# DeltaNet's triangular inverse: update products that serve two chunks, and a block transposition on VectorE

## The chip, the cores and the metric

The kernel runs on one core of one Trainium2 chip. The metric is the device time of one execution in microseconds; of the kernel before, three executions were timed, 1096.20, 1097.21 and 1097.26, median 1097.21. A further execution was profiled.

## The reference, cut to what matters

One layer of a decoder trunk: RMSNorm, one projection `z = h @ W_in`, four token mixers side by side (HGRN2, mLSTM, windowed attention, gated DeltaNet), a gated merge, an output projection and a squared-ReLU MLP. 512 tokens, model width 1024, all in float32. The change touches the DeltaNet mixer (4 heads, key and value width 128):

```
lower = where(strict, beta * (k k^T) * decay, 0) + I          # unit lower triangular, per chunk and head
sol   = triangular_solve(lower, [v*beta, k*beta*exp(gam)])    # u, w
v_new = u - w @ S;  o = q_dec @ S + attn @ v_new;  S = g_last*S + k_dec^T @ v_new    # chunk after chunk
```

The kernel uses chunks of 128 tokens (4 of them) and forms the inverse of `lower` instead of solving.

## The kernel before, in words

**Streams and tasks.** Every projection is a chain of matmuls whose weights come from memory in pieces (`raw`), are split into two reduced-precision parts `whi` (ScalarE) and `wlo` (VectorE) by `split` (L477), and go through TensorE as three 128x512 products per weight block (`mm3`). These are the streams (`pf`, `pt`, `pbr`, `yo`, `dn` in the profile). Between them lie the mixers' tasks: `dn_pre`, four `dn_head`, four `dn_fin`, four `hg_head` and so on.

**Who sets the order.** No operation is issued where it is written. The wrapper in `wrap` (the call at L223; the matmuls at L434 and transposes at L475) records each operation with an estimated cost; `lay_out` (L231) then plans all engines with these costs, at most `WINDOW = 5` tasks at a time, stream matmuls ranked behind the tasks' matmuls, and tiles taken from a fixed number of slots (`z2`: 37, `pm` in PSUM: 5, `w8`: 4). `emit` issues the operations in the planned order. On the chip each engine runs its list in that order and waits on semaphores.

**The inverse.** `dn_pre` (L930) makes `W` (the negated strict lower part, transposed) for all heads, inverts the 32x32 diagonal blocks by a serial recurrence on VectorE, and puts the result into `U0`, one tile of 16 (head, chunk) blocks of 128x128, named `dnU` in the profile. In `dn_head` (L1018) `U` is the head's part of it: the transposed inverse so far, block diagonal at first, and `Tm` its transpose by 32x32 blocks (`V.transpose`, L1025). Two doublings, n = 32 and n = 64 (L1043), fill in the off-diagonal blocks. Each does, for all four chunks:

- `yp`: four 128x128 float32 products `W^T Tm`; `Yt` is `yp` times a mask (L1045), a VectorE instruction over 128x512;
- `up`: four products `Yt^T U` (L1048); `Un = up + U`, a VectorE instruction over 128x512 into a new tile;
- for n = 32 alone, `tp`: four products `U^T Yt` (L1052) and `Tn = tp + Tm`, so that the transpose follows.

`bank4` (L792) runs the four products of one group into one PSUM bank. A float32 product of 128x128 stands as two MATMUL records in the profile. Behind the doublings comes the scan over the four chunks (`dnt`, `dno`, `dnX`, `dnV`, `dnS`), which uses `U` as an operand. `hg_head` (L1161) fills its 32 and 64 wide blocks with products that serve two chunks, and moves the wanted blocks by VectorE copies over 32 or 64 partitions (`A5`, L1212).

**The end.** `mlp_units` (L1675): the last accumulation group of the down projection is evacuated by two `scalar_tensor_tensor` of 256 columns (L1707), and each half is stored by a DMA that SyncE issues (L1712).

Of the kernel before, what the change touches and what calls it, by code (L numbers as in the profile page):

```python
# [20 lines left out]
P = 128  # L21
# [68 lines left out]
class _Flow:  # L90
# [85 lines left out]
    def wrap(self, key, eng):  # L176
        flow = self

        class W:
            def __getattr__(self, name):  # L180
                fn = getattr(eng, name)

                def call(*a, **k):
                    ops = dict(k)
                    if "out" not in ops:
                        ops["out"], a = a[0], a[1:]
                        call_a = (ops["out"],) + a
                    else:
                        call_a = a
                    out = ops.pop("out")  # L190
                    outs = [out] + ([ops.pop("accum_out")] if "accum_out" in ops else [])
                    ins = [v for v in list(a) + list(ops.values()) if isinstance(v, bass.AP)]
                    n = 1
                    for d in out.shape[1:]:
                        n *= d
                    big = [v for v in ins if v.space == PSUM]
                    table, dma = None, 0
                    if name == "dma_start":
                        dma = n * out.shape[0] * 4
                        c = 1000 if key == "g" else 500 if key == "y" else 60  # L200
                    elif key == "v":
                        if name == "tensor_tensor_scan":
                            c = 65 + 2.09 * n
                        elif name == "reciprocal":
                            c = 65 + 6.26 * n
                        elif name in ("tensor_copy", "tensor_scalar", "memset") and not big:
                            c = 65 + 0.52 * n
                        elif name in ("reduce_sum", "reduce_max"):
                            m = 1
                            for d in ins[0].shape[1:]:  # L210
                                m *= d
                            c = 65 + 1.04 * m
                        else:
                            c = 65 + 1.04 * n
                        if name in ("tensor_scalar", "scalar_tensor_tensor") and len(ins) > (1 if name == "tensor_scalar" else 2):
                            c += 65
                    elif key == "s":
                        f = a[1] if name == "activation" and len(a) > 1 else k.get("func")
                        table = {AF.Exp: "e", AF.Ln: "e", AF.Sigmoid: "s", AF.Silu: "u"}.get(f)
                        c = (52 if big else 92) + 0.833 * n + 95 * ("accum_out" in k) + 93 * sum(isinstance(k.get(x), bass.AP) for x in ("scale", "bias"))  # L220
                    else:
                        c = 110 + n * (0.8 if name == "memset" else 2.15 if len(ins) > 1 else 1.0)
                    flow.record(key, c, lambda: fn(*call_a, **k), outs, ins, table, dma,  # L223
                                two="accum_out" in k)

                return call

        return W()
# [176 lines left out]
def tile_hybrid_parallel_gated_mixers(  # L405
# [62 lines left out]
    def ch(ap, c):  # L468
        return ap[:, c * P:(c + 1) * P]
# [322 lines left out]
    def bank4(name, fn):  # L792
        o = ps(name)
        for c in range(NCH):
            fn(c, ch(o, c))
        return o
# [221 lines left out]
    def dn_head(h):  # L1018
        yield ["dnpre", f"dnv{h}"]
        q, k, v = dn["q"][h], dn["k"][h], dn["v"][h]  # L1020
        col, gl = dn["col"], dn["gl"]
        W = dn["W"][:, 4 * h:4 * h + 4, :]
        U = dn["U0"][:, 4 * h:4 * h + 4, :].rearrange("p c t -> p (c t)")
        Tm = z2("Tm")
        V.transpose(Tm, U)  # L1025
        yield
        ra = row_tile("ra", dn["ra"], h)
        qk = bank4("qk", lambda c, o: mm(o, ch(k, c), ch(q, c)))
        da, qd = z2("da"), z2("qd")
        for c in range(NCH):  # L1030
            stt(ch(da, c), ch(ra, c), col[:, c, h:h + 1], con("minc"), ALU.add, ALU.add)
        act(qd, ra, AF.Exp)
        act(da, da, AF.Exp)
        tt(qd, qd, q, ALU.mult)
        tt(da, qk, da, ALU.mult)
        yield
        kt = transpose4("kt", k)
        kd, bv = z2("kd"), z2("bv")
        tt(c3(kd), c3(kt), col[:, :, 96 + h:97 + h].to_broadcast([P, NCH, P]), ALU.mult)
        vt = transpose4("vt", v)  # L1040
        tt(c3(bv), c3(vt), col[:, :, 64 + h:65 + h].to_broadcast([P, NCH, P]), ALU.mult)
        yield
        for n in (32, 64):  # L1043
            yp = bank4("yp", lambda c, o: mm(o, W[:, c, :], ch(Tm, c)))
            Yt = z2("Yt")  # L1045
            tt(c3(Yt), c3(yp), con4(f"y{n}"), ALU.mult)
            yield
            up = bank4("up", lambda c, o: mm(o, ch(Yt, c), ch(U, c)))  # L1048
            Un = z2("U")
            tt(Un, up, U, ALU.add)  # L1050
            if n < 64:
                tp = bank4("tp", lambda c, o: mm(o, ch(U, c), ch(Yt, c)))  # L1052
                Tn = z2("Tm")
                tt(Tn, tp, Tm, ALU.add)
                Tm = Tn
            U = Un
            yield
        o, tb = ps("dno"), ps("dnt")
        St = None
        for c in range(NCH):  # L1060
            if c == 0:
                X = ch(bv, 0)
            else:
                kS = ch(tb, 0)
                mm(kS, ch(k, c), St)
                X = sq128("dnX")
                stt(X, kS, col[:, c, 32 + h:33 + h], ch(bv, c), ALU.mult, ALU.add)
                yield
            vp = ch(tb, 1)
            mm(vp, ch(U, c), X)  # L1070
            vn = sq128("dnV")
            S.copy(vn, vp)
            yield
            if c < NCH - 1:
                dS = ch(tb, 2)
                mm(dS, ch(kd, c), vn)
                Sn = sq128("dnS")
                if c == 0:
                    V.tensor_copy(Sn, dS)
                else:  # L1080
                    stt(Sn, St, gl[:, h, c:c + 1], dS, ALU.mult, ALU.add)
            if c:
                mm(ch(o, c), St, ch(qd, c), start=True, stop=False)
            mm(ch(o, c), vn, ch(da, c), start=c == 0, stop=True)
            if c < NCH - 1:
                St = Sn
                yield
        dn["on"][h] = yield from head_norm(o)
# [586 lines left out]
    def mlp_units():  # L1675

        for hf in range(NH):
# [11 lines left out]
            for j in range(2):  # L1689
                obox = {}  # L1690
                for kg in range(FH // 4):
                    r0 = (hf * FH + kg * 4) * P
                    subs = []
                    for k2 in range(2):
                        box = {}

                        def view(raw, k2=k2):
                            return raw[:, 2 * k2:2 * k2 + 2, :]

                        def step(k, c, kg=kg, k2=k2, box=box, obox=obox, hf=hf, j=j, ah=ah, al=al):  # L1700
                            kk = kg * 4 + k2 * 2 + k
                            if kk == 0 and c == 0:
                                obox["o"] = [ps("dn") for _ in range(4)]
                            o = obox["o"][c]
                            mm3(o, ch(ah[kk], c), ch(al[kk], c), box["hi"][:, k, :], box["lo"][:, k, :],
                                kk == 0, kk == FH - 1)
                            n = 2 if kk == FH - 1 and hf == NH - 1 and j == 1 and c == 3 else 1  # L1707
                            for a in range(n if kk == FH - 1 else 0):
                                cs = slice(a * T // n, (a + 1) * T // n)
                                stt(acc[c][j][:, cs], o[:, cs], tail["rs2"][:, c:c + 1], acc[c][j][:, cs], ALU.mult, ALU.add)  # L1710
                                if hf == NH - 1:
                                    Y.dma_start(out[c * P:(c + 1) * P, j * T + cs.start:j * T + cs.stop], acc[c][j][:, cs])  # L1712

                        order = [(k, c) for k in range(2) for c in range(4)]
                        if kg == FH // 4 - 1 and k2 == 1:
                            order = [(k, c) for c in range(4) for k in range(2)]
                        subs.append((pieces_k(box, view, 2, T), [lambda k=k, c=c, step=step: step(k, c) for k, c in order],
                                     None))
# [92 lines left out]
```

## Time and profile before

| what | value |
|---|---|
| median of 3 executions | 1097.21 us (1096.20 to 1097.26) |
| profiled execution | 1096.43 us, span from first to last instruction 1094.6 us |
| TensorE busy | 1081.7 us, 99% |
| VectorE, ScalarE, GpSimd busy | 678.4, 535.6, 30.2 us |
| chain that ended last | TensorE 79%, VectorE 12%, ScalarE 5% |

PE is TensorE's matmuls, PEld its weight loads, DVE VectorE, ACT ScalarE, POOL GpSimd, SP SyncE; a q behind the name is an engine's sequencer. Busy time counts a record from its start to its modelled end; matmuls overlap one another, so the distance of their starts, and not the duration of one, says how fast they follow. Back-to-back VectorE instructions overlap too: two of 0.69 us stand as one piece of about 1.28 us.

### The profile page before, as it was taken

The page shows a single profiled execution, that of the slowest core. Times are in us where ns is not written, and L with a number is a line of the kernel's source. Part 1 is how long each engine was busy: PE and PEld are TensorE (multiplying, and loading weights), DVE is VectorE, ACT ScalarE, POOL GpSimd, SP SyncE. Part 2 cuts the span into 40 slices and gives each one's busy share as a digit, 9 for nine tenths or more (in the row PEclk, how much of TensorE's full clock was granted, in tenths as well). Part 3 has the DMA queues.
Part 4 walks back from the last instruction along what each step waited for, and adds up shares of the span by engine and source line. Part 5 has one row for each costly group of instructions (what it writes and reads, how often), then busy time and mean ns, then how long its engine had stood idle before and what let it go on. Part 6 is the DMA issues. An engine that isn't in the chain of part 4 may idle for free.

```text
span 1094.6 us, 14138 instructions
## 1 busy us (share of the span) xinstructions
PE 1081.7 (99%) x5339; PEld 905.9 (83%) x5339; DVE 678.4 (62%) x1417; ACT 535.6 (49%) x970; POOL 30.2 (3%) x69
## 2 busy tenths in 40 slices
PE   8999999999999999999999999999999999999998
PEld 8889888898888888778887888888888888888886
DVE  5765999758999999976387334545443324444232
ACT  5764478226774778776267233345442222443220
POOL 4000000000000001000000010000000000000000
PEclk8999999999999999999999999999999999999999
DMA  6342554515422355222322252323232323232331
GB/s 235 89 107 97 157 182 153 185 49 167 142 87 87 108 170 174 78 78 78 116 78 77 83 186 91 102 77 116 77 116 77 116 77 116 78 115 80 113 116 39
DMA packets 95580, 122.19 MB, mean 112 GB/s; under 512 B 11104, under 2 KB 65844, under 8 KB 95256
## 3 DMA queue, kind: packets, MB, share of 16 engines
q1 hardware_dynamic: 90216, 115.03, 32.3%
q0 software_dynamic: 1984, 5.61, 1.6%
q10 hardware_dynamic: 3312, 0.66, 0.3%
q8 instruction: 42, 0.69, 0.3%
q14 instruction: 26, 0.21, 0.1%
HBM read 110.74 MB, written 12.11 MB: 112 GB/s over the span
## 4 chain that ended last, share of the span: by engine, by line
PE 79%; DVE 12%; ACT 5%; issue 2%; DMA 1%; SPq 0%; DVEq 0%; ACTq 0%
PE pf L434 41%; PE dn L434 16%; PE pbr L434 6%; PE yo L434 4%; PE pt L434 4%; DVE wlo L223 2%; DVE hG L223 2%; DVE hA L223 1%; ACT whi L223 1%; ACT L223 1%; ACT L400 1%; PE dnt L434 1%; DMA raw<-in_w_in_dram 1%; PE yp L434 1%; PE up L434 1%
## 5 line engine op out<-in xcount | busy, mean ns | idle before, releaser
L223 DVE TENSOR_TENSOR wlo<-raw,whi 128x512 fp32r<-128x512 f32 (+1 forms) x340 | 224.1, 686 | 224.9 <-ACT whi L223 224.5
L223 ACT ACTIVATE whi<-raw 128x512 fp32r<-128x512 f32 (+1 forms) x340 | 199.1, 625 | 286.0 <-PE dn L434 121.7
L434 PE MATMUL pf<-hT_lo,whi 128*128 128x512 f32 (+1 forms) x568 | 220.3, 388 | 0.3 <-DVE hT_lo L223 0.3
L434 PE MATMUL pf<-hT_hi,whi 128*128 128x512 f32 (+1 forms) x568 | 219.8, 387 | 0.0
L434 PE MATMUL pf<-hT_hi,wlo 128*128 128x512 f32 (+1 forms) x568 | 219.3, 386 | 0.0
L434 PEld LDWEIGHTS pf<-hT_lo,whi 128*128 128x128 f32 x568 | 107.4, 189 | 19.2 <-DVE hT_lo L223 0.6
L434 PEld LDWEIGHTS pf<-hT_hi,whi 128*128 128x128 f32 x568 | 107.5, 189 | 18.8
L434 PEld LDWEIGHTS pf<-hT_hi,wlo 128*128 128x128 f32 x568 | 107.4, 189 | 18.2
L434 PE MATMUL pf<-h_hi,whi 128*128 128x512 f32 x256 | 99.8, 390 | 0.0
L434 PE MATMUL dn<-whi,uh 128*128 128x512 f32 x256 | 99.6, 389 | 0.0
L434 PE MATMUL dn<-wlo,uh 128*128 128x512 f32 x256 | 99.6, 389 | 0.0
L434 PE MATMUL dn<-whi,ul 128*128 128x512 f32 x256 | 99.6, 389 | 0.0
L434 PE MATMUL pf<-h_hi,wlo 128*128 128x512 f32 x256 | 99.4, 389 | 0.0
L434 PE MATMUL pf<-h_lo,whi 128*128 128x512 f32 x256 | 99.4, 389 | 0.0
L223 DVE TENSOR_SCALAR ur<-pf 128x512 f32<-128x512 f32 x32 | 22.1, 692 | 71.5 <-PE pf L434 71.5
L434 PEld LDWEIGHTS pf<-h_hi,wlo 128*128 128x128 f32 x256 | 48.1, 188 | 10.1
L434 PEld LDWEIGHTS dn<-wlo,uh 128*128 128x128 f32 x256 | 48.1, 188 | 10.0
L434 PEld LDWEIGHTS dn<-whi,ul 128*128 128x128 f32 x256 | 48.1, 188 | 10.0
L434 PEld LDWEIGHTS pf<-h_lo,whi 128*128 128x128 f32 x256 | 48.1, 188 | 9.9
L434 PEld LDWEIGHTS pf<-h_hi,whi 128*128 128x128 f32 x256 | 48.1, 188 | 9.9
L434 PEld LDWEIGHTS dn<-whi,uh 128*128 128x128 f32 x256 | 48.1, 188 | 9.9
L223 ACT ACTIVATE gate<-pf 128x512 f32<-128x512 f32 x32 | 19.2, 601 | 67.0 <-PE pf L434 66.8
(389 smaller groups left out, 1786.3 us busy)
## 6 DMA issues: line engine op xcount, KB each, us to landing
raw<-in_w_in_dram SPq DMA_DIRECT2D x41, 1024.0 KB, 5.0
raw<-in_w_up_dram SPq DMA_DIRECT2D x16, 1024.0 KB, 5.1
raw<-in_w_down_dram SPq DMA_DIRECT2D x16, 1024.0 KB, 4.9
raw<-in_w_branch_dram SPq DMA_DIRECT2D x8, 1024.0 KB, 4.9
raw<-in_w_out_dram SPq DMA_DIRECT2D x4, 1024.0 KB, 4.9
xt<-in_x_dram SPq DMA_DIRECT2D x4, 512.0 KB, 7.4
acc<-in_x_dram POOLq DMA_DIRECT2D x8, 256.0 KB, 4.8
out_dram<-acc SPq DMA_DIRECT2D x7, 256.0 KB, 2.2
```

What stands on the lines that cost most here:

```text
L223: flow.record(key, c, lambda: fn(*call_a, **k), outs, ins, table, dma, two="accum_out" in k)
L400: self.nc.scalar.preload_act_table_set("natural_log_exp_and_others")
L434: fl.record("pe", c, lambda: nc.tensor.matmul(o, lhsT, rhs, start=start, stop=stop), [o], [lhsT, rhs], two=rhs.dtype == F32)
```

## The change

For each doubling, `Yt` holds only the columns of `yp` that the mask keeps, two chunks side by side in 128 columns, so a product of `Yt` with the second halves of the blocks of `U` in two chunks (128 columns, in runs of 32 or 64) serves both: two `up` products where there were four. The blocks of the result that belong to one chunk alone are copied from PSUM into `U` in place, by four copies over 32 partitions (n = 32) or two over 64 partitions (n = 64). The product `tp` and its addition go; instead VectorE transposes the new 32x32 block of each chunk from `U` into `Tm`. `Yt` is made by two instructions of 128 columns instead of one of 512. The planner adds 90 ns to its estimate of VectorE and ScalarE operations over 32 to 64 partitions. At the very end the last evacuation is cut at 384 columns instead of 256, and its second store is issued by ScalarE's queue instead of SyncE's.

```diff
+                    if key in "vs" and not dma and 32 <= out.shape[0] <= 64:
+                        c += 90
                     flow.record(key, c, lambda: fn(*call_a, **k), outs, ins, table, dma,
...
+        U3, T3 = c3(U), c3(Tm)
         for n in (32, 64):
-            yp = bank4("yp", lambda c, o: mm(o, W[:, c, :], ch(Tm, c)))
-            Yt = z2("Yt")
-            tt(c3(Yt), c3(yp), con4(f"y{n}"), ALU.mult)
+            nq = 64 // n
+            yp = c3(bank4("yp", lambda c, o: mm(o, W[:, c, :], ch(Tm, c))))
+            Yt = z2("Yt", shape=(P, 2, P))
+            for i in range(2):
+                cs = slice(2 * i, 2 * i + 2)
+                tt(Yt[:, i, :].rearrange("p (q c j) -> p q c j", q=nq, c=2),
+                   yp[:, cs, :].rearrange("p c (q u j) -> p q c u j", q=nq, u=2)[:, :, :, 0, :],
+                   con(f"y{n}").rearrange("p (q u j) -> p q u j", q=nq, u=2)[:, :, 0:1, :].to_broadcast([P, nq, 2, n]), ALU.mult)
             yield
-            up = bank4("up", lambda c, o: mm(o, ch(Yt, c), ch(U, c)))
-            Un = z2("U")
-            tt(Un, up, U, ALU.add)
+            up = ps("up", (P, 2, nq, 2, n))
+            for i in range(2):
+                rhs = U3[:, 2 * i:2 * i + 2, :].rearrange("p c (q u j) -> p q c u j", q=nq, u=2)[:, :, :, 1, :]
+                mm(up[:, i], Yt[:, i, :], rhs)
+            Uv = U.rearrange("p (i c q u j) -> p i c q u j", i=2, c=2, q=nq, u=2)
+            for q_ in range(nq):
+                for c in range(2):
+                    at0 = (2 * q_ + c) * n
+                    V.tensor_copy(Uv[2 * q_ * n:(2 * q_ + 1) * n, :, c, q_, 1, :], up[at0:at0 + n, :, q_, c, :])
             if n < 64:
-                tp = bank4("tp", lambda c, o: mm(o, ch(U, c), ch(Yt, c)))
-                Tn = z2("Tm")
-                tt(Tn, tp, Tm, ALU.add)
-                Tm = Tn
-            U = Un
+                V.transpose(T3[n:2 * n, :, 0:n], U3[0:n, :, n:2 * n])
             yield
...
-                            n = 2 if kk == FH - 1 and hf == NH - 1 and j == 1 and c == 3 else 1
-                            for a in range(n if kk == FH - 1 else 0):
-                                cs = slice(a * T // n, (a + 1) * T // n)
+                            end = (0, 3 * P, T) if hf == NH - 1 and j == 1 and c == 3 else (0, T)
+                            for a in range(len(end) - 1 if kk == FH - 1 else 0):
+                                cs = slice(end[a], end[a + 1])
                                 stt(acc[c][j][:, cs], o[:, cs], tail["rs2"][:, c:c + 1], acc[c][j][:, cs], ALU.mult, ALU.add)
                                 if hf == NH - 1:
-                                    Y.dma_start(out[c * P:(c + 1) * P, j * T + cs.start:j * T + cs.stop], acc[c][j][:, cs])
+                                    (S if cs.start else Y).dma_start(
+                                        out[c * P:(c + 1) * P, j * T + cs.start:j * T + cs.stop], acc[c][j][:, cs])
```

## Rows read from the trace of the kernel before

**Rows 1.** The page, busy time of each engine, its share of the span, its instructions.

```profile
PE 1081.7 (99%) x5339; PEld 905.9 (83%) x5339; DVE 678.4 (62%) x1417; ACT 535.6 (49%) x970; POOL 30.2 (3%) x69
```

**Rows 2.** Stretches: length, then busy time of PE, PEld, DVE, ACT, POOL; clock, DMA.

```profile
0.00:25.00 25.00, 20.45 (x132) 19.92 (x132) 14.40 (x45) 15.25 (x37) 10.19 (x23) 0.86 0.74 257
25.00:1085.00 1060.00, 1055.57 (x5186) 881.62 (x5185) 660.90 (x1369) 520.33 (x934) 19.98 (x47) 1.00 0.34 108
...
211.00:262.00 51.00, 51.00 (x356) 46.73 (x355) 33.88 (x65) 14.69 (x32) 0.00 (x0) 1.00 0.27 92
300.00:480.00 180.00, 177.09 (x959) 144.50 (x958) 166.71 (x427) 135.82 (x244) 7.25 (x20) 1.00 0.35 113
...
745.00:830.00 85.00, 85.00 (x376) 70.41 (x375) 41.16 (x64) 36.26 (x63) 0.00 (x0) 1.00 0.30 94
```

**Rows 3.** The chain that ended last: start, length in us, what, and how many.

```profile
219.66 0.89 PE up L434 x8
220.56 0.89 PE yp L434 x8
222.34 0.89 PE tp L434 x8
...
306.07 2.09 DVE hG L223 x6
308.16 1.20 DVE wlo L223 x2
...
743.80 85.71 PE pf L434 x378
829.51 87.04 PE dn L434 x384
```

**Rows 4.** Matmul records of the tiles up and tp: ns min/median/max, first and last start.

```profile
L434 PE MATMUL up<-dnU,Yt x32: 270/275/275, 215.0 to 244.7; 128*128 128x128 f32 x32
L434 PE MATMUL up<-U,Yt x32: 270/275/275, 221.3 to 261.4; 128*128 128x128 f32 x32
L434 PE MATMUL tp<-Yt,dnU x32: 271/275/275, 215.9 to 254.6; 128*128 128x128 f32 x32
```

**Rows 5.** VectorE's groups in the doublings: busy us, mean ns of one, idle before.

```profile
L223 DVE TENSOR_TENSOR Yt<-yp,cm 128x512 f32<-128x512 f32 x8 | 5.2, 684 | 0.6 <-PE yp L434 0.6
L223 DVE TENSOR_TENSOR U<-up,U 128x512 f32<-128x512 f32 x4 | 2.8, 691 | 2.6 <-PE up L434 2.6
L223 DVE TENSOR_TENSOR Tm<-tp,Tm 128x512 f32<-128x512 f32 x4 | 2.7, 682 | 0.4 <-PE tp L434 0.4
L223 DVE STREAM_TRANSPOSE Tm<-dnU 128x512 f32<-128x512 f32 x4 | 2.7, 692 | 1.4 <-DMA dnU<-dnd 1.4
```

**Rows 6.** VectorE's timeline in hg_head: start, length of the merged piece, instruction.

```profile
313.99 1.43 DVE L223 TENSOR_TENSOR hG<-hG,hx 128x256 f32<-128x256 f32 x4
315.33 1.29 DVE L223 TENSOR_TENSOR wlo<-raw,whi 128x512 fp32r<-128x512 f32 x2
...
317.82 0.91 DVE L223 COPY hA<-hg 32x64 f32<-32x64 f32 x4
...
320.09 0.61 DVE L223 COPY hA<-hg 64x128 f32<-64x128 f32 x2
```

**Rows 7.** VectorE on the tiles hgf and hG: ns min/median/max, first and last start.

```profile
L223 DVE SCALAR_TENSOR_TENSOR on<-on,vec,hgf x4: 733/738/741, 367.3 to 387.7; 128x512 f32<-128x512 f32 x4
...
L223 DVE TENSOR_TENSOR hG<-hG,hx x48: 405/415/426, 272.4 to 366.4; 128x256 f32<-128x256 f32 x48
```

**Rows 8.** The last microseconds, timeline of VectorE and of SyncE's queue.

```profile
1090.67 0.88 DVE L223 SCALAR_TENSOR_TENSOR acc<-dn,rs,acc 128x256 f32<-128x256 f32 x2 [0.61 <-PE dn L434]
1091.18 0.81 SPq L223 DMA_DIRECT2D out_dram<-acc  x2
```

**Rows 9.** DMA issues: KB each, median us to landing.

```profile
out_dram<-acc SPq DMA_DIRECT2D x7, 256.0 KB, 2.2
out_dram<-acc SPq DMA_DIRECT2D x2, 128.0 KB, 1.9
dnU<-dnd ACTq DMA_DIRECT2D x2, 64.0 KB, 2.1
```

## Prediction

> **What bounds the kernel now.** I read the busy shares first: TensorE is busy for 1081.7 of 1094.6 us, VectorE for 62%, ScalarE for 49% [rows 1]. A busy share alone doesn't prove a bound, so next come the stretches and the chain. Between 25 and 1085 us TensorE lacks only 1060.00 - 1055.57 = 4.43 us, with the granted clock at full speed; the rest of its idle time lies at the start, 4.55 us, and behind the last matmul [rows 2]. In the second half the chain is TensorE alone, and 384 stream matmuls take 87.04 us, 0.2267 us from start to start [rows 3]. Whatever work is taken off this list makes it shorter, as long as other work is ready in its place.
>
> The change sits in the four `dn_head`, between 211 and 262 us. There TensorE is busy for all 51.00 us, VectorE for 33.88, and ScalarE for 14.69 [rows 2], and the chain runs from matmul to matmul of this very code [rows 3]. So this stretch is bound by TensorE, and VectorE has a third of it free. The stretch behind it is different: from 300 to 480 us VectorE is busy for 166.71 of 180 us, TensorE lacks 2.91 us [rows 2], and the chain goes along VectorE's `hG` and `wlo` [rows 3]. Both engines are near their limit there; that decides one of the rivals.
>
> **The change part by part.** *TensorE.* Eight records of one group of four products take 0.89 us in the chain [rows 3], so a record is worth 0.89/8 = 0.1117 us. `up` has 32 + 32 records and `tp` has 32 [rows 4]. `up` keeps half, `tp` goes: 32 + 32 = 64 records fewer, 64 x 0.1117 = **7.15 us**. `yp` stays. A new `up` product still has 128 stationary and 128 moving columns, so I take the old price for it. The moving operand now lies in runs of 32 or 64 words, which no row shows; below nothing is excluded, since a product of 128 columns is what the cheapest of these rows already is, and the upper end is a rival below.
>
> *VectorE.* Per head go two masked `Yt`, two additions into `U` and one into `Tm`, five instructions of 128x512 at 0.68 to 0.69 us [rows 5]. Back to back they follow at 1.29 - 0.69 = 0.60 us [rows 6], so 3.0 us of the engine. In their place come four maskings of 128x128: four instructions of 256 columns fill 1.43 us [rows 6], about 0.34 from start to start, against 0.60 for 512, so 1 ns a column and 0.34 - 0.13 = 0.21 for 128; four make 0.84 us. Four copies over 32 partitions of 64 elements from PSUM exist already in `hg_head`: 0.91 us. Two of 64x128: 0.61 us [rows 6]. A transposition of 32x128 is not shown; its ends are a 32x64 copy (0.23) and the transposition of 128x512 (0.69 [rows 5]), and I take 0.30, near the 64x128 copy, which has its columns. Together 2.66 us, some 0.3 us less per head, or -1.4 us over four heads; with the upper end of the transposition 3.05, +0.2 us over four heads. Either way it is hidden under TensorE, which is the only full engine in this stretch; if VectorE were full there, these microseconds would count as they stand, up to +0.2.
>
> *What waits for what.* Per head, the matmuls of the doublings shrink from 5 x 0.89 to 0.89 + 0.45 + 0.89 + 0.45 us, and the VectorE work between them stays at 2.8 us: before `Yt`, `Tm`, `Yt`, `U` at 0.69 each, now 0.5 + 0.91 + 0.30 + 0.5 + 0.61. What is late next is the second `yp`, which waits for four copies and the transposition instead of the addition into `Tm`; behind the waiting copies on VectorE's list stand the splits `wlo` and the other heads' `dnX` and `dnS`. Stream matmuls whose weights are already split are the cover. A head's chain gets shorter, not longer, so the scans start earlier and VectorE's full stretch begins earlier by about what TensorE saves. The three `z2` tiles per head that are no longer taken cost nothing and may let a task in sooner; I count zero. `U0` lives on to the end of the scans; the next tiles of its kind are filled by `hg_fin`, behind an instruction at 367.3 us [rows 7], so zero too.
>
> *The planner.* The 90 ns are no time on the chip, but change the order on every engine. They are true to the rows: copies over 32 partitions follow at 0.23 us where the old estimate is 65 + 1.04 x 64 = 132 ns. What a new order does to TensorE's small gaps is unknown; I take zero, and for the ends the whole idle time between 25 and 1085 us, gone or doubled: -4.4 and +4.4 us.
>
> *The tail.* Before, the two last evacuations end at 1090.67 + 0.88 = 1091.55, and the second issue is over at 1091.99 [rows 8]. Cut at 384, the first ends 0.13 later and the second at the same time, since the columns are the same. Its 64 KB land 2.1 us after an issue from ScalarE's queue, against 1.9 for 128 KB from SyncE's [rows 9]: +0.2 at the worst, and -0.1 if the smaller transfer and the free queue count. SyncE's longer first issue can't delay the second any more. ScalarE has nothing behind it. I take zero.
>
> The sum: 1096.43 - 7.15 = 1089.28 us for the profiled execution. That one lies 0.78 us below the median shown, so the forecast for a median is **1090.1 us**, with the unknown order and the small terms from 1085.6 to 1094.7. About 0.2% (2.2 us) is what a measurement of this kernel can tell from no change.
>
> **The rivals.** *Half of it is given back.* From 300 to 480 us VectorE sets the chain. If the heads' end does not move forward as TensorE's list does, because a scan's steps wait for VectorE or because the new held-up copies sit ahead of `wlo`, the microseconds saved come back as gaps of TensorE there. For it: 2.91 of the 4.43 us of gaps lie in this stretch. Against it: TensorE fills every such gap with streams, and the heads' chain is shorter. With half given back: 1097.2 - 3.6 = 1093.6 us. Chance 11%.
>
> *TensorE has room left, and nothing comes of it.* Then the removed matmuls leave gaps of 7.15 us, and the time stays at 1097.2. For it: weight loads fill only 83% of the span [rows 1]. Against it: a stretch whose chain is TensorE alone, 378 matmuls in 85.71 us [rows 3], shows weight loads for 70.41 of 85 us [rows 2], 83% as well, so that share is what a full TensorE looks like here. Chance 8%. (The Trainium skill, Perfetto Trace Analysis, Identifying the Most-Contended Engine, calls the matmuls' busy time a bad metric and asks for the weight loads' share; by that rule a sixth of TensorE would be free, but the trace disagrees: 83% stands beside matmuls at their full rate.)
>
> *The scattered moving operand is slow.* Should TensorE read runs of 32 or 64 words more slowly than a row of 128, the 16 new `up` products (32 records x 0.1117 = 3.57 us at the old rate) cost k times that. The saving is gone at k = 1 + 7.15/3.57 = 3; at k = 4 the kernel is 3 x 3.57 - 7.15 = 3.6 us slower, 1100.8 us. For it: no matmul of the trace reads so. Against it: nothing in the trace shows an operand's layout to matter, and the `hG` instructions, whose blocks are just as scattered for VectorE, in widths from 2 to 64, take 405 to 426 ns [rows 7], one duration for all. Chance 6%.
>
> That the change doesn't do what it says can be read off the code: two products where four stood, and no `tp`. No chance is given to it.
>
> **How the numbers follow.** My forecast has 75%, half given back 11%, nothing 8%, slower 6%. The first two are faster by over 0.2% (below 1095.0): 0.86; same 0.08; slower 0.06. The range 1085.6 to 1094.7 holds nearly all of the first two, less the tails of the unknown order, about 8 in 10.
>
> **What would show it.** Right: `up` with 32 records and no `tp`; TensorE's busy time near 1074.5 us; 16 copies of 32x64 and 8 of 64x128 into `U` (named `dnU`) at 0.22 and 0.29 us; four transpositions of 32x128; TensorE still without gaps between 211 and 255 us, `hG` starting some 5 to 7 us earlier; TensorE's idle time from 25 us to the last matmul still near 4.4 us. Wrong: `up` records further than 0.112 us apart (third rival); TensorE's gaps between 300 and 480 us grown from 2.9 towards 6.5 us (first); the gaps in the heads' own stretch, before `yp` and behind `U`'s copies (second).

## The result, and the profile after

The changed kernel takes 1084.42 us (median of four executions, 1082.75 to 1085.09) against 1097.24 us before: ratio 0.9888, interval 0.9876 to 0.9900. It is faster by 12.8 us, where 7.1 were forecast; the time lies below the range, which began at 1085.6. In two of the runs further down one execution of four was slow (1535.75 us for the changed kernel without the planner's estimate, 3839.94 us for it with 75 ns), so their times here are the medians of the other three, 1090.94 and 1082.90 us, where the texts recorded in between reckon with 1091.4 and 1083.4.

The page, busy time of each engine in the changed kernel (before: [rows 1]); the profiled execution took 1085.04 us, span 1083.3 us:

```profile
PE 1070.7 (99%) x5275; PEld 899.0 (83%) x5275; DVE 676.7 (62%) x1441; ACT 534.7 (49%) x970; POOL 30.0 (3%) x69
```

64 matmul records fewer, 24 VectorE instructions more, VectorE's busy time down by 1.7 us. But TensorE's busy time fell by 11.0 us, not by 7.15. So more than the removed products is gone from it; what that is, the stretches show (columns as in [rows 2]):

```profile
25.00:1075.00 1050.00, 1046.76 (x5134) 877.27 (x5133) 659.81 (x1394) 520.23 (x936) 20.59 (x49) 1.00 0.34 109
...
211.00:262.00 51.00, 51.00 (x328) 45.69 (x327) 35.00 (x97) 17.36 (x38) 0.00 (x0) 1.00 0.29 97
300.00:480.00 180.00, 177.26 (x970) 148.26 (x969) 169.47 (x422) 132.23 (x239) 6.51 (x17) 1.00 0.36 117
```

TensorE still lacks nothing in the heads' stretch. From 300 to 480 us its idle time is almost unchanged (2.74 us against 2.91), but in the same 180 us it now gets through 970 matmul records instead of 959, and the weight loads are busy for 3.8 us longer. Here is what the busy share hides: a stream matmul is drawn 0.39 us long in the trace and follows its neighbour at 0.2267 us, so up to 0.16 us can be lost between two of them without leaving idle time. The number of records in a stretch shows such losses, the busy time doesn't.

The new pieces, the tile views of `up` and `Tm`, and then VectorE's timeline in the heads:

```profile
L436 PE MATMUL up<-dnU,Yt x32: 270/275/276, 215.2 to 252.0; 128*128 128x128 f32 x32
...
L225 DVE COPY dnU<-up x24: 196/225/295, 216.0 to 253.6; 32x64 f32<-32x64 f32 x16, 64x128 f32<-64x128 f32 x8
...
L225 DVE STREAM_TRANSPOSE Tm<-dnU x8: 301/485/711, 210.6 to 224.1; 128x512 f32<-128x512 f32 x4, 32x128 f32<-32x128 f32 x4
```

```profile
217.28 0.94 DVE L225 COPY dnU<-up 32x64 f32<-32x64 f32 x4
218.24 0.30 DVE L225 STREAM_TRANSPOSE Tm<-dnU 32x128 f32<-32x128 f32 x1
...
219.88 1.28 DVE L225 TENSOR_TENSOR Yt<-yp,cm 128x128 f32<-128x128 f32 x6
221.23 0.61 DVE L225 COPY dnU<-up 64x128 f32<-64x128 f32 x2
```

The scattered moving operand costs nothing (275 ns a record, as in [rows 4], and the chain below has eight records in 0.89 us). Four copies take 0.94 us, the transposition 0.30, two wide copies 0.61, within 0.03 us of the estimates; six maskings stand as one piece of 1.28 us, 0.21 us apiece as estimated. The chain, columns as in [rows 3]:

```profile
215.36 0.89 PE up L436 x8
218.28 0.89 PE yp L436 x8
...
307.92 3.02 DVE hG L225 x9
...
732.49 85.71 PE pf L436 x378
992.28 87.05 PE dn L436 x384
```

The chain still runs through `hG` behind 300 us and through TensorE alone from 732 us on. The first `hG` of all, in the tile view of `hG`, changed kernel and then the kernel before:

```profile
L225 DVE TENSOR_TENSOR hG<-hx x48: 406/417/458, 261.5 to 362.4; 128x256 f32<-128x256 f32 x48
```

```profile
L223 DVE TENSOR_TENSOR hG<-hx x48: 397/414/460, 267.7 to 363.2; 128x256 f32<-128x256 f32 x48
```

It starts 6.2 us earlier, but that is not what the time hangs on: with 180 and 270 ns in the planner (below) the changed kernel's first `hG` starts at 266.4 and 271.8 us, and the kernel is faster still. The tail, timeline as in [rows 8]:

```profile
1078.93 0.39 PE L436 MATMUL dn<-whi,ul 128*128 128x512 f32 x1
1079.35 0.88 DVE L225 SCALAR_TENSOR_TENSOR acc<-dn,rs,acc 128x384 f32<-128x384 f32 x2 [0.61 <-PE dn L436]
1080.26 0.39 ACTq L225 DMA_DIRECT2D out_dram<-acc  x1
```

The two evacuations take 0.88 us as before, and the issue of the last store is over 1.30 us after they began (1080.26 + 0.39 - 1079.35), before 1.32. From their beginning the span has 3.95 us left, before 3.93.

### The profile page after: what moved, and what is told of

It reads as the page before. It is cut to its first block, busy times and chain, and to the rows that moved or that the text cites. A ratio compares the mean times of both kernels' runs of the same rounds, so it can differ in the third digit from the quotient of the medians.

```text
span 1083.3 us, 14005 instructions
## 1 busy us (share of the span) xinstructions
PE 1070.7 (99%) x5275; PEld 899.0 (83%) x5275; DVE 676.7 (62%) x1441; ACT 534.7 (49%) x970; POOL 30.0 (3%) x69
## 4 chain that ended last, share of the span: by engine, by line
PE 86%; DVE 9%; DMA 2%; issue 1%; ACT 1%; SPq 0%; DVEq 0%; ACTq 0%
PE pf L436 46%; PE dn L436 16%; PE pbr L436 7%; PE yo L436 4%; PE pt L436 4%; DVE wlo L225 2%; DVE hG L225 1%; DVE hA L225 1%; PE dnt L436 1%; PE hg L436 1%; PE yp L436 1%; PE apt L477 1%; PE aov L436 1%; PE dno L436 1%; PE mo L436 1%
## 5 line engine op out<-in xcount | busy, mean ns | idle before, releaser
L436 PE MATMUL pbr<-brh,wlo 128*128 128x512 f32 x128 | 50.3, 393 | 0.0
```

The source lines that it names most:

```text
L436: fl.record("pe", c, lambda: nc.tensor.matmul(o, lhsT, rhs, start=start, stop=stop), [o], [lhsT, rhs], two=rhs.dtype == F32)
```

## The experiments

Every time below is a median. The kernel before was timed beside each group of runs, at 1096.1 to 1096.8 us, against 1097.24 beside the changed kernel; the ratios are to it. So differences across groups are good to about 1 us.

### The change split in two: the planner's estimate and the rest

The kernel before with two lines added, no work changed:

```diff
+                    if key in "vs" and not dma and 32 <= out.shape[0] <= 64:
+                        c += 90
```

> The kernel before with the planner's 90 ns alone; the work is the same on every engine. The change gained 12.8 us where 7.15 us of matmuls went. Theory A (the truer estimate gives an order with fewer gaps on TensorE, and that is the missing 5 to 6 us): about 1092 us against 1097. Theory B (the gaps close because of the DeltaNet edit itself: its shorter chain and lighter TensorE list): 1097, no change. Theory C (any change of the plan moves the gaps by some us, in either direction): anything from 1091 to 1101, unlike A's figure only by chance.

Measured: 1089.18 us, ratio 0.9928 (0.9912 to 0.9945). The two lines that cost nothing on the chip are worth 7.3 us. Theory B falls. Theory A has the direction, but its figure (1092) was 3 us too high. And the changed kernel without them:

> The changed kernel without the 90 ns in the planner. Theory A: only the matmuls' 7.15 us are left of the gain, about 1090 us. Theory B: 1084 to 1085 us, as the changed kernel. Theory C: 1084 to 1094, and its distance from the changed kernel does not mirror that of the cost alone.

Measured: 1090.94 us, ratio 0.9949 (0.9933 to 0.9966). The edit of the inverse alone is worth 5.5 us, the estimate on top of it 6.5. So the part of the gain that I had not forecast is the planner's, and the two parts add up: 5.5 + 7.3 = 12.8, as measured.

Where does it come from? The kernel with the two lines and the kernel before have the same 5339 matmul records. The stretches of both; first the kernel before, in two stretches that stand nowhere above, then the kernel with the estimate alone:

```profile
285.00:500.00 215.00, 211.99 (x1131) 173.43 (x1130) 197.22 (x498) 162.05 (x294) 7.45 (x21) 1.00 0.36 115
...
620.00:1060.00 440.00, 440.00 (x1958) 364.49 (x1957) 186.96 (x289) 149.78 (x266) 4.26 (x8) 1.00 0.32 104
```

```profile
285.00:500.00 215.00, 213.90 (x1163) 180.29 (x1162) 201.73 (x507) 157.72 (x298) 7.06 (x20) 1.00 0.37 117
300.00:480.00 180.00, 178.90 (x986) 150.85 (x985) 172.04 (x438) 130.86 (x248) 6.86 (x19) 1.00 0.37 118
620.00:1060.00 440.00, 440.00 (x1958) 364.52 (x1957) 183.40 (x284) 148.70 (x264) 4.26 (x8) 1.00 0.31 103
```

Late in the kernel nothing differs: 1958 records in 440 us, both times. From 285 to 500 us TensorE gets through 1163 records of the same work instead of 1131. 32 stream matmuls at 0.2267 us would be 7.3 us, and the span is 6.8 us shorter (1087.8); TensorE's idle time fell by only 1.9 us. The rest was lost time that the busy share hides. A count from the two traces shows it directly: take every distance from one matmul's start to the next, less the usual distance for that pair of shapes. By this estimate some 15.5 us are lost between 300 and 480 us before, and some 9.7 us with the planner's estimate. The losses lie where VectorE is fullest, and where the 32 and 64 wide blocks of `hg_head` and much of the attention's work over 64 partitions stand. A look at that kernel's VectorE there:

```profile
449.23 1.52 DVE L225 SCALAR_TENSOR_TENSOR aqT<-aqp,qg,aqT 64x512 fp32r<-64x512 f32 x2
450.77 1.45 DVE L225 SCALAR_TENSOR_TENSOR ak<-akp,vec,ak 64x128 fp32r<-64x128 f32 x4
...
466.21 0.85 DVE L225 TENSOR_TENSOR aos<-aov,aos 64x256 f32<-64x256 f32 x2
```

One of the first takes 0.76 us, and the old estimate gives 65 + 1.04 x 512 + 65 = 662 ns; one of the second 0.36 against 263; one of the last 0.43 against 331. Each is some 100 ns longer than planned. I take it that TensorE's list therefore held matmuls at places where their operands came late; no run shows this step by itself. In full-width work the overlap of about 0.08 us with the next instruction makes the old estimate right ([rows 6]: 0.34 us from start to start where it says 331 ns).

The number of partitions is not what decides it. In the kernel before, the update of `mC` over 64 partitions starts, by the code of `ml_head`, at partition 0 for one head and at 64 for the next:

```profile
385.01 0.33 DVE L223 SCALAR_TENSOR_TENSOR mC<-mC,mdec,mot 64x128 f32<-64x128 f32 x1
385.27 1.27 DVE L223 TENSOR_TENSOR mD<-msp,mD 128x512 f32<-128x512 f32 x2
...
392.11 0.35 DVE L223 SCALAR_TENSOR_TENSOR mC<-mC,mdec,mot 64x128 f32<-64x128 f32 x1
392.49 1.29 DVE L223 TENSOR_TENSOR wlo<-raw,whi 128x512 fp32r<-128x512 f32 x2
```

The first overlaps the next instruction by 0.07 us (385.01 + 0.33 - 385.27), the second ends 0.03 us before it. So the flat 90 ns are too much for some of the operations that they are added to.

(The Trainium skill, VectorE: DVE Perf Modes, Two Vector instructions with no wait between them, states a model in which an instruction is held until all earlier ones have finished if an input or its output starts in another group of 32 partitions than the last one in that memory. The trace agrees: the overlap is lost in the rows of `aqT`, `ak` and `aos`, whose blocks start at 0 and 64 in turn, and at 392.11 us, and is kept at 385.01 us.)

### Whose operations, and how long

> The changed kernel with the planner's 90 ns on VectorE's operations alone. VectorE has 138 operations over 32 to 64 partitions, ScalarE 57, and VectorE is the fuller engine from 300 to 480 us. Theory A: most of the 7 us, 1085 to 1087. Theory C: anywhere from 1083 to 1093.

```diff
-                    if key in "vs" and not dma and 32 <= out.shape[0] <= 64:
+                    if key == "v" and not dma and 32 <= out.shape[0] <= 64:
```

Measured: 1084.81 us, ratio 0.9894 (0.9880 to 0.9907): all of it.

> The changed kernel with the planner's 90 ns on ScalarE's operations alone. Theory A: the smaller part, 1089 to 1091 us, and the two parts together about 7. Theory C: anywhere from 1083 to 1093, and the two parts do not add up.

```diff
-                    if key in "vs" and not dma and 32 <= out.shape[0] <= 64:
+                    if key == "s" and not dma and 32 <= out.shape[0] <= 64:
```

Measured: 1090.77 us, ratio 0.9951 (0.9935 to 0.9966), against 1090.94 without any: nothing. It is VectorE's estimate, and theory A's split holds.

The next text names a theory D, which came up behind the run with 180 ns (further down): a longer estimate puts slack between VectorE's results and their users, and more slack is better.

> The changed kernel with a truer estimate still: the flat 90 ns go, and the planner adds 90 ns to an operation of VectorE or ScalarE whose operands start in another group of 32 partitions than those of the operation that it planned before it on that engine, whatever the number of partitions. In the trace of before, overlap with the neighbour is lost there and nowhere else. Theory A: at least as good as 90, 1080 to 1084 us. Theory D: between 0 and 90 or as 90, 1084 to 1090, as the slack added is about the same. Theory C: anything from 1080 to 1092.

```diff
-                    if key in "vs" and not dma and 32 <= out.shape[0] <= 64:
-                        c += 90
...
+                if o[12]:
+                    at0 = last_q[e]
+                    cost += 90 * any(at0.get((w, m), s) != s for w, m, s in o[12])
+                    for w, m, s in o[12][::-1]:
+                        at0[w, m] = s
```

Here `o[12]` holds, for each operand, whether it is written, whether it lies in PSUM, and the group of 32 partitions in which it starts. Measured: 1084.22 us, ratio 0.9883 (0.9866 to 0.9900). An estimate that follows the start and not the number of partitions does as well as the flat 90 ns, not better. Theory D allowed this figure, theory A's range ended 0.2 us below it, and C's holds it too. Its trace says more than its time. From 300 to 480 us it is much better than the changed kernel's 970 records:

```profile
300.00:480.00 180.00, 179.96 (x991) 151.34 (x990) 171.17 (x428) 132.87 (x237) 7.05 (x19) 1.00 0.36 117
```

But TensorE stands still for 2.2 us before the first `yp` of the heads, behind a load of `dnU` that took 5.7 us where the changed kernel's took 2.4. (Overlap is also lost where an instruction uses the result of the one before it; "nowhere else" in the text above passes over those.)

> The changed kernel with 180 ns instead of 90 in the planner. Theory A: the estimate is now as wrong as it was, in the other direction, so 1086 to 1090 us. Theory B: 1084 to 1085. Theory C: moves by up to 4 us in either direction.

```diff
-                        c += 90
+                        c += 180
```

Measured: 1080.04 us, ratio 0.9850 (0.9836 to 0.9865). No theory had this (C, with up to 4 us, came nearest): 4.4 us better still, with an estimate that is now too long. So more steps were run, on both codes, each with this one number changed:

> The changed kernel with 75 ns in the planner in place of 90, a shift too small to matter for any reason but chance. Theory A (the estimate is worth what it is true; 0 gave 1091.4, 90 gave 1084.4): 1084 to 1086 us. Theory D (a longer estimate puts slack between VectorE's and ScalarE's results and their users, and more is better; 180 gave 1080.0): 1085 to 1086. Theory C (the plan's luck): off the line between 0 and 90, which is at 1085.6, by 2 us or more.

Measured: 1082.90 us, ratio 0.9878 (0.9861 to 0.9894). That is below the ranges of A and D and more than 2 us off the line, as only theory C had it.

> The changed kernel with 270 ns in the planner, three times what the traces show to be lost. Theory A: worse than 180, back to 1084 us or above. Theory D: no worse than 180, 1078 to 1081. Theory C: no order between 90, 180 and 270 by size.

Measured: 1079.41 us, ratio 0.9842 (0.9828 to 0.9857). Theory A in the form that the truest figure is the best falls; D's range holds the time.

> The kernel before with 180 ns in the planner (90 gave 1089.2). If the step from 90 to 180 is worth 4.4 us whatever the code (A or D): about 1084.8 us, and the DeltaNet edit is worth 4.8 us there too. Theory C: not 1084.8 but anything from 1084 to 1093. If the edit is worth its full 7.15 us once the gaps are small: 1087.2.

Measured: 1090.39 us, ratio 0.9943 (0.9928 to 0.9958): on the old code 180 is no better than 90. At that point the scatter from plan to plan looked like the answer, and four more steps were run:

> The changed kernel with 135 ns in the planner. On it 90 gave 1084.4 and 180 gave 1080.0. If a longer estimate helps steadily on this code: about 1082 us. If the step is a matter of which plan one happens to get: off 1082 by 2 us or more.

Measured: 1082.90 us, ratio 0.9875 (0.9860 to 0.9889), within 1 us of the figure for a steady effect.

> The kernel before with 45 ns in the planner; 0 gave 1096.5 and 90 gave 1089.2. If the gain grows with the truth of the estimate: about 1093 us. If any plan other than the old one is as good (the old one being an unlucky plan): 1089 to 1090 already.

Measured: 1093.72 us, ratio 0.9974 (0.9964 to 0.9985). Not any new plan will do: half the estimate gives under half the gain, near the 1093 named.

> The kernel before with 270 ns in the planner; 90 gave 1089.2 and 180 gave 1090.4, while the changed kernel gained 5 us from 90 to 270. If that further gain belongs to the longer estimate: 1085 us or less. If it is the changed kernel's own plan: 1088 to 1091.

Measured: 1086.79 us, ratio 0.9912 (0.9895 to 0.9928): between the two figures. The longer estimate helps here too, by less than on the changed kernel.

> The kernel before with 75 ns in the planner, beside the changed kernel with 75 (1083.4). The edit of the inverse is worth the difference of the two: with its full 7.15 us 1090.5, with the 5 us seen at 0 and at 90 1088.4.

Measured: 1091.44 us, ratio 0.9954 (0.9939 to 0.9969), so the edit is worth 8.5 us at 75 ns, above both figures.

| planner's addition, ns | code before | changed code | the edit's worth |
|---|---|---|---|
| 0 | 1096.47 | 1090.94 | 5.5 |
| 45 | 1093.72 | | |
| 75 | 1091.44 | 1082.90 | 8.5 |
| 90 | 1089.18 | 1084.42 | 4.8 |
| 135 | | 1082.90 | |
| 180 | 1090.39 | 1080.04 | 10.4 |
| 270 | 1086.79 | 1079.41 | 7.4 |

Down each column the time falls with the addition, by about 7 us up to 90 ns and by 2.4 (before) and 5.0 us (changed) from there to 270, with 1 to 2 us of scatter on the way. Across the rows the edit is worth 5.5, 8.5, 4.8, 10.4 and 7.4 us, 7.3 in the mean. That agrees with the 7.15 us of the sum, but loosely: the scatter from pair to pair is some 2 us, so the mean of five is good to about 1 us.

The further gain from 90 to 270 ns lies in the same stretch. Here are the changed kernel with 180 and with 270 ns, then the kernel before with 270:

```profile
300.00:480.00 180.00, 180.00 (x988) 152.34 (x987) 168.06 (x409) 132.39 (x232) 6.86 (x18) 1.00 0.37 118
300.00:480.00 180.00, 179.72 (x996) 152.13 (x995) 166.42 (x393) 127.13 (x211) 7.17 (x20) 1.00 0.38 122
300.00:480.00 180.00, 180.00 (x989) 152.53 (x989) 163.80 (x388) 126.75 (x215) 7.25 (x20) 1.00 0.37 119
```

TensorE's idle time there is gone or nearly so, with 988 and 996 records in place of 970, and 989 in place of 959.

### The price of a matmul

> The changed kernel with the 32 removed products put back as dead work: per head two more products at each doubling and four more at n = 32, written to PSUM and read by nobody. 64 records x 0.1117 us = 7.15 us of TensorE. If a matmul record is worth its time in the end, 1084.4 + 7.15 = 1091.6 us, and the remaining gain of 5.6 us over the kernel before is not the matmuls' (A and C agree with that). Theory B in the form that the lighter TensorE list closes the gaps: 1096 to 1097 us.

```diff
+            dead = ps("dead", (P, 2, P))
+            for i in range(2):
+                mm(dead[:, i, :], Yt[:, i, :], ch(U, i))
+            if n < 64:
+                tp = bank4("tp", lambda c, o: mm(o, ch(U, c), Yt[:, c // 2, :]))
```

Measured: 1088.13 us, ratio 0.9925 (0.9910 to 0.9940), +3.7 us. This is a miss for the full price, but the planner had made a new plan around the dead products, so price and plan are mixed. The next run keeps the order:

> The changed kernel with its order untouched: each up product is issued four times (n = 32) or twice (n = 64) into the same place, outside the planner's knowledge, so that TensorE has the 64 records back and every other instruction stands where it stood. The price of a matmul record free of any new order. Full price: 1084.4 + 7.15 = 1091.6 us. If part of the saved TensorE time had turned into gaps behind it (the rival in which some is given back), part is absorbed now: 1088 to 1090. The replanned version of this, which put the products back for the planner too, gave 1088.1.

```diff
-    def mm(o, lhsT, rhs, start=True, stop=True):
+    def mm(o, lhsT, rhs, start=True, stop=True, times=1):
...
-        fl.record("pe", c, lambda: nc.tensor.matmul(o, lhsT, rhs, start=start, stop=stop), [o], [lhsT, rhs],
-                  two=rhs.dtype == F32)
+        fl.record("pe", c, lambda: [nc.tensor.matmul(o, lhsT, rhs, start=start, stop=stop) for _ in range(times)],
+                  [o], [lhsT, rhs], two=rhs.dtype == F32)
...
-                mm(up[:, i], Yt[:, i, :], rhs)
+                mm(up[:, i], Yt[:, i, :], rhs, times=4 if n < 64 else 2)
```

Measured: 1091.90 us, ratio 0.9958 (0.9945 to 0.9970), 7.5 us above the changed kernel and 7.3 above the run without the tail, which stood beside it on the same chip (below). The tile view shows the records that are back:

```profile
L436 PE MATMUL up<-dnU,Yt x96: 271/275/275, 213.9 to 257.9; 128*128 128x128 f32 x96
```

There are 96 where the changed kernel has 32, so 64 more: 7.15 us by the sum, 7.3 to 7.5 measured. In a fixed order a matmul record in the heads costs its full 0.112 us, at the end of the kernel too; this run shows nothing absorbed by the stretch where VectorE is full.

### The tail

> The changed kernel with the tail of the kernel before: last evacuation cut at 256, both stores from SyncE's queue. The order of everything else is the same, instruction for instruction. My step counted zero, bounds -0.1 to +0.2: 1084.4 us within 0.3.

```diff
-                            end = (0, 3 * P, T) if hf == NH - 1 and j == 1 and c == 3 else (0, T)
-                            for a in range(len(end) - 1 if kk == FH - 1 else 0):
-                                cs = slice(end[a], end[a + 1])
+                            n = 2 if kk == FH - 1 and hf == NH - 1 and j == 1 and c == 3 else 1
+                            for a in range(n if kk == FH - 1 else 0):
+                                cs = slice(a * T // n, (a + 1) * T // n)
...
-                                    (S if cs.start else Y).dma_start(
-                                        out[c * P:(c + 1) * P, j * T + cs.start:j * T + cs.stop], acc[c][j][:, cs])
+                                    Y.dma_start(out[c * P:(c + 1) * P, j * T + cs.start:j * T + cs.stop], acc[c][j][:, cs])
```

Measured: 1084.63 us (1083.60 to 1085.55), ratio 0.9891 (0.9878 to 0.9905), against 0.9888 with the tail. Worth nothing that this measurement can tell.

## Why the prediction was wrong

**The sum for TensorE was right.** 64 records at 0.1117 us went, the new products have the old price, and at a fixed order they are worth 7.3 to 7.5 us. The bound that I read (TensorE alone in the second half, TensorE full in the heads) holds: what is taken off its list in the heads comes off the end. The sign that I gave for it does not: TensorE's busy time was to be near 1074.5 us and is 1070.7, since a better order also takes away lost time that counts as busy (with the estimate alone and all 5339 records it is 1076.9 us against 1081.7).

**VectorE, the order of waits and the tail were right.** The maskings, copies and transpositions took their estimates; the transposition, which the trace of before did not show, 0.301 us for the 0.30 taken. `hG` starts 6.2 us earlier, within the 5 to 7 named, though the planner's new order is in that number too, and with 180 and 270 ns it starts later at a shorter time; that sign came true in part by luck. The tail is zero.

**The step that failed is the planner.** I wrote that the 90 ns "are no time on the chip, but change the order on every engine", that what a new order does "is unknown; I take zero", with ends of -4.4 and +4.4 us. It is worth -7.3 us alone and -6.5 with the edit. Two things were wrong in it. First, even odds: I had seen that the old estimate misses by 100 ns in work that stands where VectorE is 93% full and sets the chain [rows 2, 3], and that the new one is true to the copies I looked at. That argued for a gain, which I did not count. It does not give the cause, though: 180 and 270 ns, well over the 100 ns that the rows show, gained more on the changed code. Second, the bound was too narrow, because it was TensorE's idle time, 4.43 us. In a list of matmuls that overlap, idle time counts only gaps over 0.16 us. The records show what it left out: 1131 in 215 us there, and 1163 with the better order, up to 7.3 us in that stretch alone. Before a run, the bound could not be had from that count of one order.

**The rivals.** *Half of it is given back* looked right after two pairs (5.5 and 4.8 us of 7.15), and is not: at 75, 180 and 270 ns the edit is worth as much or more, and at a fixed order its matmuls are worth all of it. Scatter of the plan is enough to explain the two. *TensorE has room left* falls as a statement about the edit, since put-back products cost their full time. But the sentence with which I set the Trainium skill's rule aside was too quick. The weight loads' share is no measure of room by itself (83% beside full rate holds), yet it saw what busy time did not: from 300 to 480 us it rose from 144.50 [rows 2] to 150.85 us with the estimate alone, while TensorE's busy time rose by 1.8 (177.09 to 178.90). (The Trainium skill, Perfetto Trace Analysis, Identifying the Most-Contended Engine, says that matmul busy share is not a good measure of the distance from roofline and names the weight loads' share instead, beside the share of peak arithmetic. Compared between these two orders of one list, the trace agrees.) *The scattered moving operand* falls: 275 ns.

**What stays open.** Why an estimate longer than the true one helps further, by 5.0 us on the changed code and 2.4 on the old from 90 to 270 ns. Where it helps is seen: from 300 to 480 us, as with the first 90 ns. Slack for VectorE in a plan that leaves it none would explain it, but so would other operations that the planner still takes as too short; no run tells these apart. For the same reason it stays open how much of the first 7.3 us comes of a truer estimate and how much of a longer one. The changed kernel with 270 ns, 1079.41 us, is the fastest seen, 5.0 us below the change as it was made.

## What to carry to other kernels

Where a planner or a hand-written order is made from estimated durations, a change of the estimates is a change of the kernel: give it a term of its own, look first where estimate and trace differ on the engine that is fullest, and run it alone. Scatter from one plan to the next was some 2 us here, so one pair of kernels does not measure an edit. To price removed work by itself, freeze the order: put the work back, outside the planner's knowledge, and compare. And where matmuls overlap, count the records in a stretch; TensorE's busy share of 98.6% hid a loss of some 5 us in 215.

## What the runs showed of the hardware that I had not expected

VectorE instructions on blocks that start at another partition than those before them lose the overlap of about 0.08 us and pay a little more: in the changed kernel four copies of 32x64, 0.22 us each, fill 0.94 us, where four full-width instructions of 256 columns and 0.415 us each fill 1.43 [rows 6]. A block of 64 partitions that starts at 0, like the full-width ones around it, keeps it (`mC`, above). A float32 matmul whose moving operand lies in scattered runs of 32 or 64 words costs as much as one with a row of 128: 275 ns a record, eight records in 0.89 us.
